# Attention scores in two PSUM banks with one maximum, one exponential and one copy for a tile, and the first key and query transposes within the projections

## The chip, the cores and the metric

The kernel runs on one core of a Trainium2 chip, as one program. The metric is device time in microseconds (us) of one execution, the median of the runs of a version. Each of the core's engines works through its own list of instructions strictly in the order in which they stand there: TensorE (PE) does matmuls and transposes, VectorE (DVE) and ScalarE (ACT) do elementwise work, reductions and copies, GpSimd (POOL) does elementwise work on SBUF, and SyncE (SP) issues most of the DMAs. An instruction at the head of a list that waits for another engine holds up all that stand behind it.

## The reference, cut to what matters

Two transformer blocks of width 1024 over 512 tokens follow one another. The change lies in the attention layer of the first block (layer 1 of 2), which has 16 query heads in 4 groups of 4 that share a key and value head, head dimension 64, and 256 context tokens in front of the 512 latent keys, 768 keys in all:

```python
qkv = h_lat @ w_qkv
q = rmsnorm(qkv[..., :Q_DIM].reshape(B, S, N_Q_HEADS, HEAD_DIM), q_g)
k = rmsnorm(qkv[..., Q_DIM:Q_DIM + KV_DIM].reshape(B, S, N_KV_HEADS, HEAD_DIM), k_g)
q, k = apply_rope(q, cos, sin), apply_rope(k, cos, sin)
kv_c = h_ctx @ w_qkv[:, Q_DIM:]              # context keys (normed, not turned) and values
k_all = jnp.concatenate([k_c, k], axis=1); v_all = jnp.concatenate([v_c, v], axis=1)
s = jnp.einsum('bqhgd,bkhd->bhgqk', q_blk * HEAD_DIM ** -0.5, k_all)
p = jax.nn.softmax(s, axis=-1)
y = jnp.einsum('bhgqk,bkhd->bqhgd', p, v_all) ... @ w_o
```

Beside it stands adaLN: `m = silu(c) @ w_mod + b_mod`, 6 x 1024 numbers that scale and shift the layer's normalized inputs. For this layer, 32 columns of 128 of them are needed only after the attention.

## The kernel before, in words

**Projections.** `gemm_tm` multiplies the token-major input by w_qkv in blocks of 512 columns: block 2 (keys and values, latent and context), then block 0 (query heads 0 to 7), then block 1 (heads 8 to 15). Weights come by DMA (`load_raw`), are split into a high part (ACT, L294) and a low part (DVE or POOL, L295), and each product is three matmuls (L353 to L355). A block of four token blocks of 128 is 192 matmuls in two weight halves, and its results leave through a handler.

**The query handler.** `q_out` takes one token block. For block 0 the chain is: square (ACT, L1597), sum (DVE, L1599), square root (ACT, L192), a few short DVE steps, scale and two rope products (DVE, L1608, L1615, L1622), rope add (POOL, L1623), high part (ACT cast, L1644), low part (POOL, L1645). For block 1 only the norm's factor is worked out and the raw values are copied (L1657); their rope follows inside the attention loop (`q_rest`, all on POOL with one ACT cast).

**Keys and queries across.** `k_stack` (L1667 to L1670) splits one key head; `k_trans` turns two token blocks of it by four PE transposes (the transposes are all L177) and casts the result (L1703); `q_trans` does the same for one query head of four token blocks (L1710). The first `k_trans` of key head 0 and `q_trans(0)`, `q_trans(1)` stand behind the projections, then eight transposes that spread silu(c) over 128 partitions (`crow`, copied by ACT, L1814).

**The attention loop.** A tile is one query head and 128 queries against 768 keys, 64 in all. In a step t the loop issues S(t), the scores (four matmuls, L1724 to L1727, in two PSUM banks of 512 and 256 columns); T(t-2), six transposes of that tile's exponentials; the maxima of t (DVE, L1733, L1734, joined at L1736); the copies out of PSUM of the transposed tile (512 columns on DVE, L1768; 256 on ACT, L1764); E(t), two exponentials with two accumulated sums (ACT, L1746, L1747); and, for each second tile, the 24 matmuls of the pair's product with the values (V, L1779). Every eight tiles a norm round divides by the sums (`norm_a` on DVE, L1787, L1788, L1790; `norm_b`, four transposes and two copies, L1800, L1801). A PSUM tile is one bank, and eight of them go round under one name, `ps`.

**AdaLN's 32 rows.** Each is a load of 512 KB (SP), a product with `crow` (POOL, L1819) and a sum (ACT, L1820). They are spread over tiles 12 to 55, each issued behind that tile's exponential.

**Order.** The code gives the order for PE within the loop; a scheduler then merges what stands in the code into one list for each engine, so that the place on ACT, DVE and POOL of work from `fill` and from the handlers is decided by it. Nothing is reordered on the chip.

Of the kernel before, what the change touches and what calls it, by code (L numbers as in the profile page):

```python
# [63 lines left out]
def build(tc, A, out, stop=None, dbg=None):  # L64
# [12 lines left out]
    psp = es.enter_context(tc.tile_pool(name="ps", bufs=8, space=bass.MemoryType.PSUM))  # L77
    drp = es.enter_context(tc.tile_pool(name="dr", bufs=1, space=bass.MemoryType.DRAM))

    ph = K()  # L80

    class phase:

# [1510 lines left out]
    def head_rstd(ps, nh):  # L1594
        w = nh * 64
        q = t2()
        S.activation(q[:, :w], ps[:, :w], AF.Square)  # L1597
        v = sm([128, nh], tag=f"hv{nh}")
        V.reduce_sum(v, q[:, :w].rearrange("p (h e) -> p h e", e=64), axis=AX.X)  # L1599
# [61 lines left out]

# [15 lines left out]
    def next_phase():  # L1677
# [7 lines left out]
    qst = [s8r() for _ in range(4)]  # L1685
    gemm_tm(wq, [0], 8, lat_h, 4, q_out)
    gemm_tm(wq, [1], 8, lat_h, 4, q_out, first=lambda: k_stack(0))


    on = [s8(), s8()]  # L1690

    def och(c):
        return on[c // 4][:, (c % 4) * 512 : (c % 4) * 512 + 512]
# [25 lines left out]
    def scores(t):  # L1719
        hd, qb = tile_of(t)  # L1720
        KT = KTs[hd // 4][1]
        qsl = QTs[hd][:, qb * 128 : qb * 128 + 128]
        pa, pb = PS(), PS()
        mm(pa, qsl, KT[:, 0:512], start=True, stop=False)  # L1724
        mm(pa, qsl, KT[:, 768:1280], start=False, stop=True)
        mm(pb[:, 0:256], qsl, KT[:, 512:768], start=True, stop=False)
        mm(pb[:, 0:256], qsl, KT[:, 1280:1536], start=False, stop=True)  # L1727
        st_[t] = [pa, pb]

    def maxima(t):  # L1730
        pa, pb = st_[t]
        mx = sm([128, 2], tag=f"amx{t % 2}")
        V.reduce_max(mx[:, 0:1], pa, axis=AX.X)  # L1733
        V.reduce_max(mx[:, 1:2], pb[:, 0:256], axis=AX.X)  # L1734
        nmx = sm([128, 1], tag=f"anm{t % 2}")
        V.tensor_scalar(nmx, mx[:, 0:1], mx[:, 1:2], -0.125, op0=ALU.max, op1=ALU.mult)  # L1736
        st_[t].append(nmx)

    def exps(t):
        hd, qb = tile_of(t)  # L1740
        pa, pb, nmx = st_[t]
        if t % 8 == 0:
            den_[hd // 2] = sm([128, 4, 2, 2], tag=f"aden{hd // 2 % 2}")
        d2 = den_[hd // 2][:, qb, hd % 2, :]
        P = hip.tile([128, 1024], F32, tag="hi", name=nm("P"))
        S.activation(P[:, 0:512], pa, AF.Exp, bias=nmx, scale=0.125, accum_out=d2[:, 0:1])  # L1746
        gate_[t] = S.activation(P[:, 512:768], pb[:, 0:256], AF.Exp, bias=nmx, scale=0.125, accum_out=d2[:, 1:2])  # L1747
        st_[t] = P

    def p_trans(t):  # L1750
        P = st_[t]
        PT = l4()
        pts = []
        for half, nk in ((0, 4), (1, 2)):
            pt = PS()
            for j in range(nk):
                kc = 4 * half + j
                transpose(pt[:, j * 128 : j * 128 + 128], P[:, kc * 128 : kc * 128 + 128])
            pts.append(pt)
        st_[t] = (PT, pts)  # L1760

    def p_evac_b(t):
        PT, pts = st_[t]
        S.copy(PT[:, 512:768], pts[1][:, 0:256])  # L1764

    def p_evac_a(t):
        PT, pts = st_[t]
        V.tensor_copy(PT[:, 0:512], pts[0])  # L1768
# [35 lines left out]
    for i in range(3):
        k_trans(0, i)
    q_trans(0)
    q_trans(1)

    crow = xc.rearrange("p c t -> p (c t)")[:, 0:1024]
    for h_ in range(2):  # L1810
        pt = PS()
        for k in range(4):
            transpose(pt[:, 128 * k : 128 * k + 128], cs[:, 4 * h_ + k, 0:1].to_broadcast([128, 128]))
        S.copy(crow[:, 512 * h_ : 512 * h_ + 512], pt)  # L1814
    adraw = {}

    def adaln_rows(j):
        w = adraw.pop(j)
        G.tensor_tensor(w, w, crow, op=ALU.mult)  # L1819
        S.activation(w, w, AF.Copy, accum_out=mod[1][:, 16 + j, 0:1])  # L1820
        if j == 31:
            m = mod[1][:, 16:48, 0]
            V.tensor_tensor(m, m, vc("b_mod", 64, 32), op=ALU.add)

    NT_ = 64
    LT, LV = 2, 3
    adt = [12 + j * 45 // 32 for j in range(32)]
    for t in range(NT_ + LV + 3):
        for j in range(32):
            if max(adt[j] - 4, 0) == t:  # L1830
                adraw[j], = load_raw(A["wmodT"][j // 2][:, j % 2 * 1024 : j % 2 * 1024 + 1024], 1024)
        if t < NT_:
            scores(t)
        if 0 <= t - LT < NT_:
            p_trans(t - LT)
# [12 lines left out]
        if u >= 8 and u % 8 == 1:  # L1848
            norm_b(u // 8 - 1)
        if t < NT_:  # L1850
            if t % 8 in (3, 5) and t < 56:
                q_trans(2 * (t // 8) + 2 + t % 8 // 5)
            kv, w = divmod(t, 16)
            if kv < 3 and w == 5:
                k_stack(kv + 1)
            if kv < 3 and w in (8, 9, 11):
                k_trans(kv + 1, {8: 0, 9: 1, 11: 2}[w])
            for j in [j for j in range(32) if adt[j] == t]:
                with tc.issue_after(gate_[t].ins), tc.issue_after(lastg[0].ins):
                    adaln_rows(j)  # L1860
# [717 lines left out]
```

## Time and profile before

| | us |
|---|---|
| median of 3 runs (lowest, highest) | 2212.08 (2210.4, 2221.37) |
| the profiled execution | 2213.96 |
| its span | 2212.1 |
| mean granted TensorE clock of it | 0.978 |
| PE, DVE, ACT, POOL busy | 2078.8, 1415.5, 1107.3, 512.2 |

The span is the time from the first to the last instruction of the trace. The busy sums are over the whole program; the change touches only the stretch from about 386 to 611 us, in which blocks 0 and 1 of the projection and the attention lie. PE is in the chain that ended last for 64% of the span. A wait in a row stands in square brackets: the idle time before the instruction, and what ended it.

### The profile page before, as it was taken

How to read it: one execution, taken by the hardware profiler on the slowest of the kernel's cores; microseconds unless marked ns; L12 is line 12 of the kernel's file. 1: busy time of each engine (PE TensorE's matmuls, PEld its weight loads, DVE VectorE, ACT ScalarE, POOL GpSimd, SP SyncE). 2: the span in 40 equal slices, each digit the busy share in tenths (PEclk: the TensorE clock that was granted, in tenths of full speed). 3: DMA queues.
4: the chain of work that ended last, by engine and by line, in shares of the span. 5: the costliest groups of instructions: out<-in, count | busy, mean ns of one | idle time of the engine just before them, and what ended most of it. 6: DMA issues, size and time to landing. Idle time of an engine off the chain costs nothing.

```text
span 2212.1 us, 32447 instructions
## 1 busy us (share of the span) xinstructions
PE 2078.8 (94%) x12305; PEld 1694.3 (77%) x12305; DVE 1415.5 (64%) x2300; ACT 1107.3 (50%) x1977; POOL 512.2 (23%) x514
## 2 busy tenths in 40 slices
PE   6869998999998999999999999999999999999997
PEld 1448767788875667776698888999878888888997
DVE  4579878678736887267757767526363568565633
ACT  3648864388836886344434434324253465343422
POOL 1011020477202313145422101014100024101011
PEclk9889999999999999999999999999999999999998
DMA  9699973124426995321123333322322213333321
GB/s 375 263 357 392 417 278 101 58 71 135 177 89 225 377 389 186 94 73 49 57 63 100 91 100 95 96 87 68 105 84 80 67 48 94 97 95 95 96 77 39
DMA packets 94096, 323.05 MB, mean 146 GB/s; under 512 B 11521, under 2 KB 17168, under 8 KB 93424
## 3 DMA queue, kind: packets, MB, share of 16 engines
q1 hardware_dynamic: 76480, 274.76, 36.5%
q0 software_dynamic: 7856, 27.92, 3.6%
q10 hardware_dynamic: 9600, 18.26, 2.3%
q8 instruction: 98, 1.61, 0.3%
q14 instruction: 62, 0.51, 0.1%
HBM read 300.63 MB, written 20.27 MB: 145 GB/s over the span
## 4 chain that ended last, share of the span: by engine, by line
PE 64%; DVE 7%; DMA 5%; POOL 3%; issue 2%; ACT 2%; DVEq 0%; POOLq 0%; ACTq 0%; SPq 0%
PE ps L353 18%; PE ps L355 18%; PE ps L354 18%; PE ps L177 3%; PE ps L1779 1%; DVE lo L295 1%; DMA s<-in_mgu_dram 1%; POOL raw L1819 1%; PE ps L2162 1%; PE ps L2313 1%; PE ps L2361 1%; DVE s L1998 1%; DMA rawx<-in_mdn_dram 1%; DVE s L1990 1%; DMA raw<-in_mgu_dram 1%
## 5 line engine op out<-in xcount | busy, mean ns | idle before, releaser
L353 PE MATMUL ps<-s,hi 128*128 128x512 f32 (+1 forms) x1440 | 512.1, 357 | 4.0 <-DVE s L1990 2.9
L354 PE MATMUL ps<-s,hi 128*128 128x512 f32 (+1 forms) x1440 | 507.4, 353 | 3.0 <-DVE s L1998 1.8
L355 PE MATMUL ps<-s,lo 128*128 128x512 f32 (+1 forms) x1440 | 508.9, 354 | 0.0
L294 ACT CAST hi<-raw 128x1024 fp32r<-128x1024 f32 x282 | 291.8, 1047 | 411.8 <-PE ps L354 330.5
L295 DVE TENSOR_TENSOR lo<-raw,hi 128x1024 fp32r<-128x1024 f32 x231 | 287.3, 1258 | 275.4 <-ACT hi L294 275.0
L295 POOL TENSOR_TENSOR lo<-raw,hi 128x1024 fp32r<-128x1024 f32 x51 | 122.9, 2409 | 870.6 <-ACT hi L294 870.6
L353 PEld LDWEIGHTS ps<-s,hi 128*128 128x128 f32 x1440 | 270.8, 188 | 46.7 <-issue 7.4
L354 PEld LDWEIGHTS ps<-s,hi 128*128 128x128 f32 x1440 | 271.6, 189 | 42.1 <-DVE s L1998 2.4
L355 PEld LDWEIGHTS ps<-s,lo 128*128 128x128 f32 x1440 | 271.6, 189 | 38.7 <-issue 0.5
L353 PE MATMUL ps<-hi,s 128*128 128x512 f32 (+1 forms) x528 | 216.7, 411 | 8.3 <-ACT hi L294 5.4
L354 PE MATMUL ps<-lo,s 128*128 128x512 f32 (+1 forms) x528 | 212.3, 402 | 2.1 <-DVE lo L295 2.1
L355 PE MATMUL ps<-hi,s 128*128 128x512 f32 (+1 forms) x528 | 211.8, 402 | 2.4 <-DVE s L1897 2.4
L355 PE MATMUL ps<-t2r,lo 128*128 128x256 f32 (+1 forms) x640 | 188.2, 294 | 0.0
L354 PE MATMUL ps<-t2r,hi 128*128 128x256 f32 (+1 forms) x640 | 187.9, 294 | 0.0
L353 PE MATMUL ps<-t2r,hi 128*128 128x256 f32 (+1 forms) x640 | 187.2, 293 | 0.0
L353 PEld LDWEIGHTS ps<-hi,s 128*128 128x128 f32 (+1 forms) x528 | 105.7, 200 | 33.7 <-ACT hi L294 7.7
L355 PEld LDWEIGHTS ps<-hi,s 128*128 128x128 f32 (+1 forms) x528 | 105.5, 200 | 28.7 <-DVE s L1897 4.0
L354 PEld LDWEIGHTS ps<-lo,s 128*128 128x128 f32 (+1 forms) x528 | 105.8, 200 | 25.0 <-DVE lo L295 2.6
L354 PEld LDWEIGHTS ps<-t2r,hi 128*128 128x128 f32 x640 | 120.8, 189 | 5.3 <-issue 2.5
L355 PEld LDWEIGHTS ps<-t2r,lo 128*128 128x128 f32 x640 | 120.8, 189 | 5.1 <-issue 2.5
L353 PEld LDWEIGHTS ps<-t2r,hi 128*128 128x128 f32 x640 | 121.1, 189 | 2.8
L295 DVE TENSOR_TENSOR lo<-s,hi 128x1024 fp32r<-128x1024 f32 x97 | 113.9, 1220 | 7.9 <-ACT hi L294 6.3
(384 smaller groups left out, 3702.8 us busy)
## 6 DMA issues: line engine op xcount, KB each, us to landing
raw<-in_up_dram SPq DMA_DIRECT2D x88, 512.0 KB
s<-in_mgu_dram SPq DMA_DIRECT2D x64, 512.0 KB
raw<-in_mgu_dram SPq DMA_DIRECT2D x44, 512.0 KB
raw<-in_down_dram SPq DMA_DIRECT2D x44, 512.0 KB
raw<-in_dilqkv_dram SPq DMA_DIRECT2D x36, 512.0 KB
s<-in_mdn_dram SPq DMA_DIRECT2D x34, 512.0 KB
raw<-in_wmodT_dram SPq DMA_DIRECT2D x32, 512.0 KB
s<-in_wmod_dram SPq DMA_DIRECT2D x30, 512.0 KB
```

What stands on the lines that cost most here:

```text
L177: return PE.transpose(dst, src, ident if idt is None else idt)
L294: S.copy(hi, raw)
L295: eng.tensor_tensor(lo, raw, hi, op=ALU.subtract)
L353: mm(ps, ahi, bhi, start=start, stop=False)
L354: mm(ps, ahi, blo, start=False, stop=False)
L355: return mm(ps, alo, bhi, start=False, stop=stop)
L1779: mm(po_[c][o : o + 64, qb * 128 : qb * 128 + 128], vview[:, kc, c // 2 * 64 : c // 2 * 64 + 64], PTs[h_][:, kc * 128 : kc * 128 + 128], s ...
L1819: G.tensor_tensor(w, w, crow, op=ALU.mult)
L1990: V.tensor_tensor(mv, mv, bc(self.rb[:, None, 0:256], [128, 2, 256]), op=ALU.mult)
L1998: V.scalar_tensor_tensor(self.h.lo(c)[:, ts], x[:, c, ts], g_, self.h.hi(c)[:, ts], op0=ALU.mult, op1=ALU.subtract)
L2162: mm(po[64 * hh : 64 * hh + 64, kb * 128 : 512], vt, at[:, o : o + n], start=(kb == 0), stop=(kb == 3), tile_position=(0, 64 * hh))
L2313: mm(pzs[hh][:, o : o + n], q.q[pp, pr * 512 + qb * 128 : pr * 512 + qb * 128 + 128], q.k[pp, pr * 512 + k1 - n : pr * 512 + k1], start=Tr ...
```

## The change

1. PSUM is laid out anew for the attention: two buffers of two banks for scores (`pz`), one of two banks for transposed tiles (`pt`), one bank for the value products (`po`) and one for the rest (`ps`). Ahead of it and behind it there are eight of one bank as before.
2. A tile has one maximum over 768 (negated in the same instruction), one exponential with one accumulated sum, and one copy, alternately by DVE (even tiles) and ACT (odd). The factor 0.125 goes into the query's gain. `norm_a` has no sum of two parts any more and its broadcast copy is on ACT.
3. Into blocks 0 and 1 of the projection come, by `fill`: the `crow` transposes, 6 of the 32 adaLN rows, the three `k_trans` of key head 0, and `q_trans(0)` and `q_trans(1)`. The other 26 rows are spread over tiles 8 to 56. Some `q_trans` and `k_trans` stand one or two tiles later.
4. The norm's factor of block 1's queries is worked out once for all four token blocks, behind the projections.

```diff
+    def PS(dt=F32, of="ps"):
+        pool, w = getattr(ph, of)
+        return pool.tile([128, 512 * w], dt, tag=of, name=nm(of))
...
+        V.tensor_scalar(qkg[:, 0, :], qkg[:, 0, :], 0.125, None, op0=ALU.mult)
...
-        rs = gsm([128, 8], tag=f"qrs{tb}")
-        V.tensor_copy(rs, head_rstd(ps, 8))
         S.copy(raw, ps)
-        qlater[tb] = (raw, rs)
+        head_sums(ps, 8, qss[:, 8 * tb : 8 * tb + 8])
+        qlater[tb] = raw
...
+    NROW = 6
+    beside = {0: [lambda: crow_half(0)], 1: [lambda: crow_half(1)]}
+    for j in range(NROW):
+        beside.setdefault(2 * j, []).append(lambda j=j: adrow_load(j))
+        beside.setdefault(2 * j + 3, []).append(lambda j=j: adaln_rows(j))
+    for i in range(3):
+        beside.setdefault(12 + i, []).append(lambda i=i: k_trans(0, i))
+    for i in range(2):
+        beside.setdefault(14 + i, []).append(lambda i=i: q_trans(i))
+    qst = [s8r() for _ in range(4)]
+    gemm_tm(wq, [0], 8, lat_h, 4, q_out, fill=next_beside, first=lambda: k_stack(0))
+    qss = gsm([128, 32], tag="qss")
+    gemm_tm(wq, [1], 8, lat_h, 4, q_out, fill=next_beside)
...
+        pz = PS(of="pz")
+        for o, n in ((0, 512), (512, 256)):
+            for p_ in (0, 768):
+                mm(pz[:, o : o + n], qsl, KT[:, p_ + o : p_ + o + n], start=p_ == 0, stop=p_ > 0)
+        st_[t] = pz[:, 0:768]
...
+        V.tensor_reduce(nmx, st_[t], axis=AX.X, op=ALU.max, negate=True)
...
-        S.activation(P[:, 0:512], pa, AF.Exp, bias=nmx, scale=0.125, accum_out=d2[:, 0:1])
-        gate_[t] = S.activation(P[:, 512:768], pb[:, 0:256], AF.Exp, bias=nmx, scale=0.125, accum_out=d2[:, 1:2])
+        gate_[t] = S.activation(P[:, 0:768], pz, AF.Exp, bias=nmx, accum_out=den_[hd // 2][:, qb, hd % 2 : hd % 2 + 1])
...
+        (S.copy if t % 2 else V.tensor_copy)(PT[:, 0:768], pt[:, 0:768])
...
-        V.tensor_tensor(rd, den[:, :, :, 0], den[:, :, :, 1], op=ALU.add)
-        V.reciprocal(rd, rd)
+        V.reciprocal(rd, den)
         rdx = t2()
-        V.tensor_copy(rdx.rearrange("p (q h e) -> p q h e", q=4, h=2),
+        S.copy(rdx.rearrange("p (q h e) -> p q h e", q=4, h=2),
...
+    banks(pz=(2, 2), pt=(1, 2), po=(1, 1), ps=(1, 1))
+    qrs = rstd_from(qss, 1.0 / 64, [128, 32], "hnq", o=gsm([128, 32], tag="qrs"))
...
-    adt = [12 + j * 45 // 32 for j in range(32)]
+    adt = {j: 8 + (j - NROW) * 50 // (32 - NROW) for j in range(NROW, 32)}
...
-                q_rest(1, t // 7, *qlater[t // 7], G)
+                q_rest(1, t // 7, qlater[t // 7], qrs[:, 8 * (t // 7) : 8 * (t // 7) + 8], G)
```

How this moves instructions shows at three places. A number behind a name is a buffer; an `x4` stands for four alike.

POOL, the list ahead of and within block 0's query chain. In before, the rope adds and low parts of the four token blocks (`t_37..`, `s_368.`) follow a weight's low part:

```order
L295 TENSOR_TENSOR lo_3761<-raw_3754,hi_3760 128x1024
L1623 TENSOR_TENSOR t_3792<-t_3793,t_3795 128x512
L1645 TENSOR_TENSOR s_3684<-t_3792,s_3684 128x8x64
L1623 TENSOR_TENSOR t_3829<-t_3830,t_3832 128x512
L295 TENSOR_TENSOR lo_3985<-raw_3978,hi_3984 128x1024
L1645 TENSOR_TENSOR s_3685<-t_3829,s_3685 128x8x64
```

In the changed kernel, the same place, where the rope add is L1637, the low part L1659, and an adaLN row's product L1732:

```order
L305 TENSOR_TENSOR lo_3780<-raw_3773,hi_3779 128x1024
L1681 COPY s_3795<-s_3795 128x6x64
L1682 TENSOR_TENSOR s_3795<-ktok,s_3795 128x6x64
L1732 TENSOR_TENSOR raw_3723<-raw_3723,xc 128x1024
L1732 TENSOR_TENSOR raw_3755<-raw_3755,xc 128x1024
L1732 TENSOR_TENSOR raw_3825<-raw_3825,xc 128x1024
L1732 TENSOR_TENSOR raw_3903<-raw_3903,xc 128x1024
L1732 TENSOR_TENSOR raw_3973<-raw_3973,xc 128x1024
L1732 TENSOR_TENSOR raw_4001<-raw_4001,xc 128x1024
L1637 TENSOR_TENSOR t_3816<-t_3817,t_3819 128x512
L1659 TENSOR_TENSOR s_3685<-t_3816,s_3685 128x8x64
L305 TENSOR_TENSOR lo_4026<-raw_4019,hi_4025 128x1024
```

All six products stand ahead of the first rope add. On ACT the sums of the first five stand ahead of the first token block's square, and the sixth between it and its square root.

PE, the end of the projections. In before the transposes of keys and queries stand behind the last matmul of token block 3 of block 1 (`ps_3915`):

```order
L355 MATMUL ps_3915<-hi_3984,s_3180 128x512
L177 MATMUL ps_4112<-ident,s_4000 128x128 x4
L177 MATMUL ps_4118<-ident,s_4000 128x128 x4
L177 MATMUL ps_4124<-ident,s_4000 128x128 x4
L177 MATMUL ps_4130<-ident,s_3684 128x128
L177 MATMUL ps_4130<-ident,s_3685 128x128
L177 MATMUL ps_4130<-ident,s_3686 128x128
L177 MATMUL ps_4130<-ident,s_3687 128x128
```

In the changed kernel the last keys (`s_3795`) and query head 0 (`ps_4098`, from all four `s_3685` to `s_3688`) stand ahead of the last twelve matmuls of token block 3 (`ps_3948`):

```order
L365 MATMUL ps_3947<-hi_4025,s_3180 128x512
L187 MATMUL ps_4092<-ident,s_3795 128x128 x4
L187 MATMUL ps_4098<-ident,s_3685 128x128
L187 MATMUL ps_4098<-ident,s_3686 128x128
L187 MATMUL ps_4098<-ident,s_3687 128x128
L187 MATMUL ps_4098<-ident,s_3688 128x128
L363 MATMUL ps_3948<-hi_4021,s_3178 128x512
L364 MATMUL ps_3948<-lo_4022,s_3178 128x512
```

So the transpose of the fourth token block of head 0 now has twelve projection matmuls behind it.

ACT, around the casts of `q_rest` (high parts of block 1's queries). In before the first of them stands behind the fifth exponential:

```order
L1764 COPY lo_4259<-ps_4265 128x256
L1746 ACTIVATE P_4275,sm_4167<-ps_4253,sm_4272 128x512
L1644 CAST s_3684<-t_4244 128x8x64
L1747 ACTIVATE P_4275,sm_4167<-ps_4254,sm_4272 128x256
L1764 COPY lo_4297<-ps_4303 128x256
L1710 CAST t2r_4321<-ps_4316 128x512
```

In the changed kernel (exponential L1794, cast L1658, copy L1806, square root L202) it stands behind the third, close behind the square root on which its input rests:

```order
L202 ACTIVATE t_4144<-g_3944,epst 128x32
L1794 ACT_TABLE_LOAD
L1794 ACTIVATE P_4161,sm_4160<-pz_4153,sm_4158 128x768
L1794 ACTIVATE P_4170,sm_4160<-pz_4163,sm_4168 128x768
L1794 ACTIVATE P_4188,sm_4160<-pz_4172,sm_4185 128x768
L1713 CAST t2r_4257<-ps_4252 128x512
L1658 CAST s_3685<-t_4210 128x8x64
L1806 COPY lo_4202<-pt_4195 128x768
```

The copy of the second tile's transposes stands behind that cast. The third such cast (`s_3687`) stands behind the seventeenth exponential; on POOL six row products, the split of a key head and four rope steps stand between the low part of `s_3686` and the rope add that it reads.

## Rows read from the trace of the kernel before

**Rows 1.** Windows. Start:end length, busy PE, PEld, DVE, ACT, POOL, granted clock, DMA share, GB/s.

```profile
386.56:431.20 44.64, 44.64 (x193) 35.96 (x192) 28.76 (x67) 15.14 (x29) 18.83 (x15) 1.00 0.22 72
431.20:443.05 11.85, 6.78 (x42) 5.77 (x40) 10.64 (x33) 7.77 (x17) 6.24 (x7) 0.86 0.00 0
443.05:610.40 167.35, 161.14 (x1520) 137.68 (x1520) 131.09 (x293) 144.01 (x416) 99.19 (x58) 0.99 0.37 128
479.08:586.56 107.48, 101.27 (x923) 84.66 (x922) 82.29 (x175) 93.89 (x267) 74.48 (x39) 0.98 0.48 162
```

**Rows 2.** Timeline of PE, 431 to 444 us. Start, duration, engine, instruction, idle before.

```profile
431.20 2.35 PE L177 MATMUL ps<-ident,s 128*128 128x128 f32 x20
...
437.90 0.50 PE L1724 MATMUL ps<-s,t2r 128*128 128x512 f32 x1 [3.48 <-ACT t2r L1710]
...
443.05 0.89 PE L177 MATMUL ps<-ident,P 128*128 128x128 f32 x6 [1.60 <-ACT P L1746]
```

**Rows 3.** Timeline of ACT, 391 to 446 us: square roots, a cast, a table load.

```profile
402.00 0.30 ACT L192 ACTIVATE sm<-sm,epst 128x8 f32<-128x8 f32 x1 [0.75 <-DVE sm L1599]
...
407.41 0.30 ACT L192 ACTIVATE sm<-sm,epst 128x8 f32<-128x8 f32 x1
...
427.36 0.62 ACT L1644 CAST s<-t 128x512 fp32r<-128x512 f32 x1 [5.26 <-POOL t L1623]
...
439.33 1.28 ACT L1746 ACT_TABLE_LOAD   x1
```

**Rows 4.** Timeline of POOL, 400 to 462 us: rope steps.

```profile
405.56 1.29 POOL L1623 TENSOR_TENSOR t<-t,t 128x512 f32<-128x512 f32 x1 [15.13 <-DVE t L1622]
407.58 1.30 POOL L1645 TENSOR_TENSOR s<-t,s 128x512 fp32r<-128x512 f32 x1 [0.73 <-PE ps L355]
...
428.06 1.29 POOL L1645 TENSOR_TENSOR s<-t,s 128x512 fp32r<-128x512 f32 x1 [0.38 <-ACT s L1644]
...
450.63 1.04 POOL L1608 TENSOR_TENSOR t<-s,g 128x512 f32<-128x512 f32 x1
...
454.50 1.29 POOL L1623 TENSOR_TENSOR t<-t,t 128x512 f32<-128x512 f32 x1
```

**Rows 5.** Timeline of PE, 481 to 491 us: scores, transposes, value products.

```profile
483.19 0.51 PE L1724 MATMUL ps<-s,t2r 128*128 128x512 f32 x1
...
484.00 0.82 PE L177 MATMUL ps<-ident,P 128*128 128x128 f32 x6
484.66 0.60 PE L177 MATMUL ps<-ident,s 128*128 128x128 f32 x4
...
486.73 1.53 PE L1779 MATMUL ps<-lo,s 128*64 128x128 f32 x24
488.19 0.66 PE L177 MATMUL ps<-ident,t 128*128 128x128 f32 x4
```

**Rows 6.** Lines by form, 437 to 612 us. Instruction and count, busy us and mean ns, idle before.

```profile
L1819 POOL TENSOR_TENSOR raw<-raw,xc 128x1024 f32<-128x1024 f32 x32 | 75.6, 2384 | 14.0 <-DMA raw<-in_wmodT_dram 9.9 <-ACT P L1747 3.6 <-ACT raw L1820 0.4
...
L1746 ACT ACTIVATE P<-ps,sm 128x512 f32<-128x512 f32 x64 | 45.1, 705 | 16.3 <-DVE sm L1736 16.0
...
L1768 DVE COPY lo<-ps 128x512 f32<-128x512 f32 x64 | 43.7, 682 | 1.7 <-PE ps L177 1.5
...
L1820 ACT ACTIVATE raw<-raw 128x1024 f32<-128x1024 f32 x32 | 34.4, 1073 | 1.7 <-POOL raw L1819 1.7
...
L1747 ACT ACTIVATE P<-ps,sm 128x256 f32<-128x256 f32 x64 | 31.0, 485 | 0.0
...
L1764 ACT COPY lo<-ps 128x256 f32<-128x256 f32 x64 | 24.6, 384 | 6.9 <-PE ps L177 6.7
...
L1669 POOL TENSOR_TENSOR s<-ktok,s 128x384 fp32r<-128x384 f32 x3 | 3.2, 1063 | 0.0
```

**Rows 7.** Timeline of DVE and of PE, 521 to 527 us.

```profile
521.54 2.13 DVE L1787 TENSOR_TENSOR sm<-sm 128x8 f32<-128x8 f32 x1
...
526.92 0.33 PE L1779 MATMUL ps<-lo,s 128*64 128x128 f32 x2 [1.71 <-DVE lo L1768]
```

More of the change, by code (lines that the diff above doesn't have):

```diff
@@ L76, in build, with banks @@
     smp = es.enter_context(tc.tile_pool(name="sm", bufs=1))
-    psp = es.enter_context(tc.tile_pool(name="ps", bufs=8, space=bass.MemoryType.PSUM))
     drp = es.enter_context(tc.tile_pool(name="dr", bufs=1, space=bass.MemoryType.DRAM))
     ph = K()
+    pse = es.enter_context(contextlib.ExitStack())
+    def banks(**n):
+        pse.close()
+        for name, (bufs, w) in n.items():
+            setattr(ph, name, (pse.enter_context(tc.tile_pool(name=nm(name), bufs=bufs, space=bass.MemoryType.PSUM)), w))
     class phase:
@@ L102, in nm @@
         return f"{p}{uid[0]}"
-    def PS(dt=F32):
-        return psp.tile([128, 512], dt, tag="ps", name=nm("ps"))
+    def PS(dt=F32, of="ps"):
+        pool, w = getattr(ph, of)
+        return pool.tile([128, 512 * w], dt, tag=of, name=nm(of))
+    banks(ps=(8, 1))
     def s8(dt=F32):
@@ L1597, in head_rstd @@
         S.activation(q[:, :w], ps[:, :w], AF.Square)
+        V.reduce_sum(v, q[:, :w].rearrange("p (h e) -> p h e", e=64), axis=AX.X)
+    def head_rstd(ps, nh):
         v = sm([128, nh], tag=f"hv{nh}")
[L1599 removed]
+        head_sums(ps, nh, v)
         return rstd_from(v, 1.0 / 64, [128, nh], f"hn{nh}")
@@ L1684, in build @@
             then=(ctx_h, 2, kv_out(0, False)))
[L1685 to L1693, printed above, removed]
     def k_trans(kvh, i):
@@ L1709, in q_trans, with crow_half, adrow_load, adaln_rows @@
         QT = t2r()
-        S.copy(QT, pt)
+        (V.tensor_copy if hd == 1 else S.copy)(QT, pt)
         QTs[hd] = QT
+    crow = xc.rearrange("p c t -> p (c t)")[:, 0:1024]
+    def crow_half(h_):
+        pt = PS()
+        for k in range(4):
+            transpose(pt[:, 128 * k : 128 * k + 128], cs[:, 4 * h_ + k, 0:1].to_broadcast([128, 128]))
+        S.copy(crow[:, 512 * h_ : 512 * h_ + 512], pt)
+    adraw = {}
+    def adrow_load(j):
+        adraw[j], = load_raw(A["wmodT"][j // 2][:, j % 2 * 1024 : j % 2 * 1024 + 1024], 1024)
+    def adaln_rows(j):
+        w = adraw.pop(j)
+        G.tensor_tensor(w, w, crow, op=ALU.mult)
+        S.activation(w, w, AF.Copy, accum_out=mod[1][:, 16 + j, 0:1])
+        if j == 31:
+            m = mod[1][:, 16:48, 0]
+            V.tensor_tensor(m, m, vc("b_mod", 64, 32), op=ALU.add)
+    NROW = 6
[7 more added lines that the diff above has]
+        beside.setdefault(14 + i, []).append(lambda i=i: q_trans(i))
+    nbeside = [0]
+    def next_beside():
+        for f in beside.get(nbeside[0], ()):
+            f()
+        nbeside[0] += 1
+    qst = [s8r() for _ in range(4)]
+    gemm_tm(wq, [0], 8, lat_h, 4, q_out, fill=next_beside, first=lambda: k_stack(0))
+    qss = gsm([128, 32], tag="qss")
+    gemm_tm(wq, [1], 8, lat_h, 4, q_out, fill=next_beside)
+    on = [s8(), s8()]
+    def och(c):
+        return on[c // 4][:, (c % 4) * 512 : (c % 4) * 512 + 512]
     st_, po_, den_, gate_ = {}, {}, {}, {}
@@ L1751, in p_trans, with p_evac @@
         P = st_[t]
[L1752 to L1768, printed above, removed]
+        pt = PS(of="pt")
+        for kc in range(6):
+            transpose(pt[:, kc * 128 : kc * 128 + 128], P[:, kc * 128 : kc * 128 + 128])
+        st_[t] = l4(), pt
+    def p_evac(t):
+        PT, pt = st_[t]
+        (S.copy if t % 2 else V.tensor_copy)(PT[:, 0:768], pt[:, 0:768])
     def pv(t):
@@ L1801, in norm_b @@
         V.tensor_tensor(och(c), po_.pop(c), rdb, op=ALU.mult)
[L1804 to L1823, printed above, removed]
+    banks(pz=(2, 2), pt=(1, 2), po=(1, 1), ps=(1, 1))
+    qrs = rstd_from(qss, 1.0 / 64, [128, 32], "hnq", o=gsm([128, 32], tag="qrs"))
     NT_ = 64
     LT, LV = 2, 3
-    adt = [12 + j * 45 // 32 for j in range(32)]
-    for t in range(NT_ + LV + 3):
-        for j in range(32):
+    adt = {j: 8 + (j - NROW) * 50 // (32 - NROW) for j in range(NROW, 32)}
+    for t in range(NT_ + LV + 2):
+        for j in adt:
             if max(adt[j] - 4, 0) == t:
-                adraw[j], = load_raw(A["wmodT"][j // 2][:, j % 2 * 1024 : j % 2 * 1024 + 1024], 1024)
+                adrow_load(j)
         if t < NT_:
@@ L1847, in build @@
                 norm_a(u // 8)
-        if u >= 8 and u % 8 == 1:
+        if u >= 8 and u % 8 == 0:
             norm_b(u // 8 - 1)
         if t < NT_:
-            if t % 8 in (3, 5) and t < 56:
-                q_trans(2 * (t // 8) + 2 + t % 8 // 5)
+            if t % 8 in (4, 6) and t < 56:
+                q_trans(2 * (t // 8) + 2 + t % 8 // 6)
             kv, w = divmod(t, 16)
@@ L1855, in build @@
                 k_stack(kv + 1)
[L1856 to L1860, printed above, removed]
+            if kv < 3 and w in (9, 10, 13):
+                k_trans(kv + 1, {9: 0, 10: 1, 13: 2}[w])
+            for j in adt:
+                if adt[j] == t:
+                    with tc.issue_after(gate_[t].ins), tc.issue_after(lastg[0].ins):
+                        adaln_rows(j)
             if t < 28 and t % 7 == 3:
-                q_rest(1, t // 7, *qlater[t // 7], G)
+                q_rest(1, t // 7, qlater[t // 7], qrs[:, 8 * (t // 7) : 8 * (t // 7) + 8], G)
+    banks(ps=(8, 1))
     phg.close()
```

29 lines of the change are left out of this document (8 added, 21 removed).

## Prediction

> **What bounds the kernel now.** I read the windows first, to cut the changed stretch into three: blocks 0 and 1 of the projection, the hand-over to the attention, the attention. [rows 1] Through the projection PE is busy 44.64 of 44.64 us: nothing is lost there, and every transpose put in between costs its own time. The hand-over, from the last projection matmul to T(0), the first transposes of exponentials, takes 11.85 us at a mean granted clock of 0.86, with PE busy 6.78. The attention takes 167.35 us from T(0) to the last value product.
>
> The timeline of PE says what the hand-over is made of [rows 2]: 28 transposes (20 of keys and queries, 8 of `crow`) from 431.20, then 3.48 us idle until the casts of queries on ACT are done, scores from 437.90, and T(0) at 443.05 behind the first exponential.
>
> For the attention the timeline gives PE's own pace at full clock, by the distance of starts [rows 5]: S 0.81 (483.19 to 484.00), T 0.66 (to 484.66), V of a pair 1.46 (486.73 to 488.19); four other transposes are 0.35 to 0.44 (0.11 each, as in T), I take 0.35. A pair of tiles is 2 x 0.81 + 2 x 0.66 + 1.46 = 4.40. Besides there are 13 query turns, 9 key turns and 8 norm rounds, 30 x 0.35 = 10.5. So PE alone needs 32 x 4.40 + 10.5 = 151.3 of the 167.35; 16 us are lost. Most of that lies in the middle: 479.08 to 586.56 is 19 pairs, 5.66 each, with ACT busy 93.9 of 107.5 us [rows 1]. There ACT is the engine to look at: a pair costs it two exponentials of two parts (2 x 1.19), two copies (2 x 0.38) and more than one row sum of 1.07 [rows 6], and the exponential then waits for a maximum that comes late (16.0 us, [rows 6]).
>
> **The change: the loop.** No operation over 768 columns stands in the trace. By the step from 256 to 512, one exponential is 0.705 + 0.22 = 0.93 (estimate; not under 0.705, not over 1.19), against 1.19 and one accumulated sum less. A copy: ACT's 256 columns take 0.384, DVE's 512 take 0.682 [rows 6], so 768 are about 0.8 on ACT and 0.95 on DVE (not under 0.68, not over 1.15). ACT's work for a pair falls from 2 x (1.19 + 0.38) = 3.1 to 2 x 0.93 + 0.8 = 2.7 and it has 26 row sums instead of 32: with one row and a third of a pair's casts 4.1 to 4.3, under PE's pace. ACT ceases to set the end.
>
> What is late next is the one buffer for transposed tiles. T of a tile can't start before the copy of the one ahead is done; before, eight banks went round and this wait didn't exist. Between two T there stand by turns one S with one matmul of V (0.87), and the rest of V with S (2.2). The copy in the shorter gap is ACT's: 0.8 and about 0.1 to get going, and up to 0.9 more if an exponential is at work. That is 0 to 0.9 for a pair; I take 0.2, near the lower end, since in the order on ACT the copy stands ahead of the next two exponentials. A pair becomes 4.60: 32 x 4.60 + 10.5 + 2 (the last tile's exponential, copy and product, which nothing covers, before as after) = 159.7, a gain of 7.6.
>
> In a norm round an addition of 8 elements took 2.13 us, and behind it PE stood idle 1.71 us for a DVE copy [rows 7]; addition and broadcast leave DVE, so such stalls go; this is part of the gain. By the Trainium skill (SBUF — State Buffer, Who interferes with whom) DVE and GpSimd hold a shared port for a whole instruction and the later one is wholly blocked, which agrees with the 2.13. The same rule speaks against six products on POOL beside the weights' low parts on DVE in the projection: by it a low part could start up to 2.38 us late, and the sum below would be up to 2 us more; no row here shows that.
>
> **The change: casts that wait on POOL.** ACT works in order; a cast of `q_rest` at its head holds up all exponentials and copies behind it. That this happens the trace shows: a cast stood 5.26 us waiting for POOL [rows 3].
> First cast. In before it had 5 tiles of time. Now it stands behind the third exponential, and its input starts only when the batched square root is there, about when the first exponential starts. POOL needs three products, a row product that stands among them, and an addition: 450.63 to 455.79 is 5.16 for the rope [rows 4], and 2.38 for the row [rows 6], 7.5. ACT gets there 3 us after: 4.5 us lost on ACT, and as much on PE, which needs the copy behind the cast.
> Third cast. POOL does between the low part of token block 1 and the rope add of 2: that low part 1.29, six rows 14.3, a key head 1.06 (without its short steps), rope 5.16 [rows 4, 6], 21.8. ACT has six tiles between the casts, three pairs 13.8 and 1.5 of turns: 15.3. Lost: 6.5. If POOL gets ahead of time in between, none; so 0 to 11 for both, and I take 11, as POOL's list is fixed and each product has a row.
> The attention then takes 159.7 + 11.0 = 170.7 against 167.35: +3.4.
>
> **The change: the hand-over.** If the queries are ready, it gains: 12 + 8 key and query transposes move inside (they cost the same there), the 3.48 idle goes; what is left behind the last matmul is the square of its result, a sum, a square root, and ACT's table load of 1.28 [rows 3]. That puts T(0) at about 439.3, 3.7 earlier.
> But six row products stand ahead of the first rope add on POOL, and the sums of five ahead of the first square on ACT. The first product needs the second `crow` copy, which ACT can do at about 396 (POOL was idle for 15.13 us before 405.56, [rows 4], so nothing else holds it). 6 x 2.38 = 14.3: the last ends at 410.3, and the first square root, 402.00 before [rows 3], comes at 412, 10 us later. From it to the end of the last low part was 402.00 to 429.35, 27.35 us [rows 3, 4]; at the least it is three periods of 5.41 (402.00 to 407.41) and a chain of 6.9 (402.00 to 408.88), 23.1. So token block 3 of the queries is ready between 435.1 and 439.4; I take 437.
> PE arrives at the transpose of query head 0 at 431.20 less twelve matmuls (44.64 / 192 x 12 = 2.8) plus 20 transposes ahead of it (2.2): 430.6. It stands there 6.4 us, and the twelve matmuls are still to come: 437.4, then 2.8 at full clock, 5.6 at half; after the idle time and the mean clock of 0.86 in the hand-over [rows 1] I take 4: 441.4. Copy and square 1.2, sum, square root and table load 2.3, exponential 0.9; scores and maximum fit beside it: T(0) at about 446.3 (443.5 to 449.5), against 443.05: +3.3.
>
> **Sum.** +3.4 + 3.3 = +6.7, and the output projection starts as late as that; with some 1 us for lower clock after the stalls, +7.7 on 2213.96, the profiled execution's own time: 2221.7. That execution is 1.9 over the median of the runs, so for the median I say 2220.
>
> **Rivals.**
> A, nothing waits on POOL: the products finish early or the chain is shorter than 18.5 us from 412, and the casts meet their inputs. Then -3.7 and -7.6: about 2201. For it speaks ACT's load in the loop, which does fall; against it the 23.1 us that the chain takes at the least.
> B, the single buffer decides: if ACT's copy of the odd tile regularly meets an exponential at work, a pair loses 0.6 instead of 0.2, 32 x 0.4 = 12.8 more: 2233. It decides from a loss of 0.35 a pair on. For it: exponential and copy are on one engine in order and 0.93 is longer than the gap; against it, the copy stands ahead of two exponentials in the list.
> C, only the casts fall away, POOL being ahead: +3.3 - 7.6 = -4.3: 2208.
>
> **How the numbers follow.** About 0.5%, 11 us, is what a measurement of this kernel can tell from no change: 2201 to 2223. My forecast 0.5, its own range 2214 to 2227; A 0.12, B 0.2, C 0.18. Half of A is faster by more than the bound, and a little more where the loop gains more than I see: 0.1. Slower: B, and the third of the forecast that lies above 2223: 0.36. The rest, 0.54, is within. The range 2203 to 2235 leaves out half of A and the far end of B.
>
> **What would show it.** Right: in PE's timeline a wait of 4 to 9 us before a transpose of queries near 431, released by POOL's low part; six row products in one block on POOL from 396 to 410; ACT idle for POOL some 4 us before the first cast of the attention and 6 before the third; pairs of 4.6 us after tile 24; exponentials of 0.9. Wrong: PE without a gap up to 433 (then A), T waiting for copies in each pair (then B), or 768 columns costing as much as the two parts, in which case ACT still sets the end and the loop gains nothing.

## The result, and the profile after

The changed kernel takes 2228.24 us (median of 6 runs, 2224.51 to 2231.93) against 2211.36 us of before, measured beside it: a ratio of 1.0070, interval 1.0052 to 1.0087, 11 to 19 us slower. The forecast of 2220 had the direction and about half of the size.

The stretch ahead of the change shifts by a few us from one execution to the next, so I count from P0, the first matmul of the attention's projections in PE's timeline: 338.02 in before, 339.61 after. T(0) lies 105.0 behind it before and 114.8 after (+9.8); from T(0) to the end of the last value product it is 167.5 before and 175.1 after (+7.6). The sum is +17.4 in these two executions; the ratio makes it 15.5.

**The hand-over.** POOL's timeline of the changed kernel (start, duration, instruction, idle before) answers to [rows 4]:

```profile
397.40 16.18 POOL L1732 TENSOR_TENSOR raw<-raw,xc 128x1024 f32<-128x1024 f32 x6
418.14 1.30 POOL L1637 TENSOR_TENSOR t<-t,t 128x512 f32<-128x512 f32 x1 [4.57 <-DVE t L1636]
...
441.19 1.27 POOL L1659 TENSOR_TENSOR s<-t,s 128x512 fp32r<-128x512 f32 x1 [0.73 <-ACT s L1658]
```

The six products stand in one block, and the first rope add comes behind it. ACT's timeline answers to [rows 3]:

```profile
414.66 0.29 ACT L202 ACTIVATE sm<-sm,epst 128x8 f32<-128x8 f32 x1
...
440.49 0.62 ACT L1658 CAST s<-t 128x512 fp32r<-128x512 f32 x1 [5.23 <-POOL t L1637]
...
449.21 0.32 ACT L202 ACTIVATE t<-g,epst 128x32 f32<-128x32 f32 x1 [0.75 <-DVE g L1609]
450.69 1.28 ACT L1794 ACT_TABLE_LOAD   x1 [1.15 <-DVE sm L1785]
451.98 0.90 ACT L1794 ACTIVATE P<-pz,sm 128x768 f32<-128x768 f32 x1
```

The first square root is 75.0 behind P0, against 64.0 before, and the last low part ends at 102.8 against 91.3. PE's timeline answers to [rows 2]:

```profile
425.74 0.76 PE L364 MATMUL ps<-lo,s 128*128 128x512 f32 x1 [3.18 <-DVE lo L305]
...
442.51 0.48 PE L187 MATMUL ps<-ident,s 128*128 128x128 f32 x1 [4.19 <-POOL s L1659]
442.64 0.78 PE L363 MATMUL ps<-hi,s 128*128 128x512 f32 x1
...
446.94 0.39 PE L365 MATMUL ps<-hi,s 128*128 128x512 f32 x1
447.18 0.60 PE L187 MATMUL ps<-ident,s 128*128 128x128 f32 x4
448.67 1.63 PE L1780 MATMUL pz<-s,t2r 128*128 128x512 f32 x8 [0.90 <-ACT t L1608]
450.14 0.60 PE L187 MATMUL ps<-ident,s 128*128 128x128 f32 x4
453.02 1.59 PE L1780 MATMUL pz<-s,t2r 128*128 128x512 f32 x4 [2.28 <-ACT P L1794]
454.42 1.48 PE L187 MATMUL pt<-ident,P 128*128 128x128 f32 x6
```

PE waits 3.18 us for a weight's low part on DVE, and 4.19 for the fourth token block's transpose. The low part's input stands behind a late query cast on ACT, and the low part itself takes 3.05 us, against 1.22 for the same one in e1 below, as POOL has begun such a subtraction just before it:

```profile
422.26 2.34 POOL L305 TENSOR_TENSOR lo<-raw,hi 128x1024 fp32r<-128x1024 f32 x1 [0.78 <-ACT hi L304]
422.63 3.05 DVE L305 TENSOR_TENSOR lo<-raw,hi 128x1024 fp32r<-128x1024 f32 x1
```

The twelve matmuls behind it follow, and the scores and T(0) behind those. S(2) at 453.02 stands ahead of T(0) and waits for the first exponential, since there are two score buffers.

**The loop.** ACT's two casts, and the PE instructions behind them:

```profile
459.83 0.62 ACT L1658 CAST s<-t 128x512 fp32r<-128x512 f32 x1 [2.64 <-POOL t L1637]
...
501.61 0.62 ACT L1658 CAST s<-t 128x512 fp32r<-128x512 f32 x1 [6.74 <-POOL t L1637]
```

```profile
461.19 0.87 PE L187 MATMUL pt<-ident,P 128*128 128x128 f32 x6 [2.05 <-ACT lo L1806]
...
502.80 0.69 PE L187 MATMUL ps<-ident,t 128*128 128x128 f32 x2 [5.70 <-ACT t L1827]
```

Three things bear on the first cast's wait, and no run parts them: it stands two exponentials further ahead; a row product of 2.39 us stands among POOL's rope steps; and POOL begins these only behind the batched square root, 2.0 us ahead of T(0), where before it began 5.0 ahead of it. The first of the steps, before and after:

```profile
438.06 1.05 POOL L1608 TENSOR_TENSOR t<-s,g 128x512 f32<-128x512 f32 x1
...
452.44 1.04 POOL L1622 TENSOR_TENSOR t<-s,g 128x512 f32<-128x512 f32 x1 [5.86 <-issue]
```

Ahead of the third cast POOL doesn't lack time either: it sat idle for ACT's second cast, and only then came the 22 us of work up to the end of the rope add (501.57):

```profile
479.41 1.29 POOL L1659 TENSOR_TENSOR s<-t,s 128x512 fp32r<-128x512 f32 x1 [12.51 <-ACT s L1658]
```

The lines of the attention by form answer to [rows 6]:

```profile
L1785 DVE TENSOR_REDUCE sm<-pz 128x1 f32<-128x768 f32 x62 | 59.3, 956 | 58.1 <-PE pz L1780 51.4 <-ACT P L1794 6.2
...
L1794 ACT ACTIVATE P<-pz,sm 128x768 f32<-128x768 f32 x64 | 57.9, 906 | 9.0 <-DVE sm L1785 8.7
...
L1806 DVE COPY lo<-pt 128x768 f32<-128x768 f32 x32 | 30.5, 952 | 13.1 <-PE pt L187 11.7
...
L1806 ACT COPY lo<-pt 128x768 f32<-128x768 f32 x32 | 25.6, 800 | 21.4 <-PE pt L187 21.4
```

One exponential of 0.906 stands where there were two of 0.705 and 0.485, and the copies take 0.80 and 0.95, as estimated. The windows answer to [rows 1]; this is the whole loop and a stretch in its second half, in which ACT has room and PE shows as busy throughout:

```profile
454.42:629.52 175.10, 164.95 (x1517) 139.66 (x1516) 99.82 (x120) 131.38 (x251) 85.32 (x54) 0.97 0.29 104
540.00:600.00 60.00, 59.95 (x558) 51.21 (x558) 35.90 (x43) 49.53 (x95) 27.13 (x13) 1.00 0.40 144
```

### The profile page after: what moved, and what is told of

It is laid out like the page before. It is cut to its first block, busy times and chain, and to the rows that moved or that the text cites. A ratio compares the mean times of both kernels' runs of the same rounds, so it can differ in the third digit from the quotient of the medians.

```text
span 2224.2 us, 32079 instructions
## 1 busy us (share of the span) xinstructions
PE 2085.6 (94%) x12305; PEld 1698.0 (76%) x12305; DVE 1379.9 (62%) x2107; ACT 1100.2 (49%) x1821; POOL 515.0 (23%) x514
## 4 chain that ended last, share of the span: by engine, by line
PE 71%; DVE 9%; DMA 7%; POOL 5%; issue 5%; ACT 3%; ACTq 0%; SPq 0%; DVEq 0%; POOLq 0%
PE ps L363 19%; PE ps L365 18%; PE ps L364 18%; PE ps L187 4%; DVE lo L305 2%; PE po L1817 2%; PE pt L187 1%; PE pz L1780 1%; POOL raw L1732 1%; DMA raw<-in_mgu_dram 1%; DMA raw<-in_wmod_dram 1%; DMA s<-in_mgu_dram 1%; PE ps L531 1%; PE ps L608 1%; PE ps L390 1%
## 5 line engine op out<-in xcount | busy, mean ns | idle before, releaser
L305 DVE TENSOR_TENSOR lo<-s,hi 128x1024 fp32r<-128x1024 f32 x97 | 113.8, 1218 | 8.3 <-ACT hi L304 6.9
```

The lines of the kernel that those rows point to most:

```text
L305: eng.tensor_tensor(lo, raw, hi, op=ALU.subtract)
```

## The experiments

P0 to T(0) and T(0) to the end are read from PE's timeline of each profiled execution; the ratio is to the kernel before, run beside it.

```
                             median   ratio   95% interval     P0-T(0)  T(0)-end
before                       2211.4   1                         105.0    167.5
changed                      2228.2   1.0070  1.0052 to 1.0087  114.8    175.1
e1  no rows beside           2218.5   1.0019  1.0001 to 1.0037  104.2    178.0
e12 three rows beside        2223.6   1.0041  1.0027 to 1.0055  109.6    179.6
e11 queries behind           2226.8   1.0055  1.0035 to 1.0075  111.5    178.8
e3  old hand-over            2214.9   1.0002  0.9985 to 1.0020  101.0    174.0
e4  old loop                 2220.2   1.0031  1.0013 to 1.0049  113.8    168.3
e2  cast later (in the code) 2225.0   1.0054  1.0036 to 1.0072  115.2    172.1
e5  cast gated               2220.2   1.0019  1.0002 to 1.0035  115.5    168.0
e6  e5, split copy           2231.8   1.0070  1.0043 to 1.0097  116.7    175.2
e7  e3, cast gated           2213.6   0.9990  0.9970 to 1.0011  102.0    172.2
e8  e7, split copy           2213.1   0.9992  0.9974 to 1.0010  102.9    173.5
e9  old hand-over, late rows 2208.8   0.9973  0.9960 to 0.9987  100.8    168.1
e10 new hand-over, late rows 2207.4   0.9970  0.9957 to 0.9984  102.2    167.3
```

**The products ahead of the query chain: e1 and e12.**

```diff
-    NROW = 6
+    NROW = 0
```

> All 32 adaLN rows back in the loop (none within the projections), the rest as changed. Theory (six products on POOL hold up block 0's query chain): first square root near 402 instead of 414.7, the waits of PE of 3.2, 0.8 and 4.2 us in block 1 go, the first transposes of exponentials (T(0)) at 440 to 443 instead of 454.4; the loop keeps its casts that wait on POOL, maybe 2 us longer with more rows in it. Time 2228 - 12 + 1 = 2217, 2212 to 2220. Rival (the single buffer for transposed tiles is what costs, the hand-over only hides in it): at least 2224.

> As changed, with three row products within the projections instead of six, the other 29 in the loop. Theory (each product holds up the query chain by its 2.4 to 2.7 us): first square root 8 us earlier and T(0) at 107 instead of 114.8; the third cast then waits for POOL 1 to 2 us longer: 2228 - 8 + 2 = 2222, 2218 to 2224. Rival (the chain is paced by something other than the products, a weight's load or low part): T(0) at 112 or later.

T(0) is 104.2, 109.6 and 114.8 behind P0 with none, three and six products: 5.4 and 5.2 for three. In e1 no wait for the queries is left, and the wait for the low part is gone too; this is its PE from the end of block 1:

```profile
435.81 0.60 PE L187 MATMUL ps<-ident,s 128*128 128x128 f32 x4
437.30 1.64 PE L1780 MATMUL pz<-s,t2r 128*128 128x512 f32 x8 [0.90 <-ACT t L1608]
438.77 0.60 PE L187 MATMUL ps<-ident,s 128*128 128x128 f32 x4
441.65 0.97 PE L1780 MATMUL pz<-s,t2r 128*128 128x512 f32 x4 [2.28 <-ACT P L1794]
```

So the products, with the sums on ACT that wait for them, are the cause of the late T(0). The size that I expected of e12 was off (8 us expected, 5.2 measured): the first square root lies 66.5, 71.2 and 75.0 behind P0 with none, three and six, so that a product moves it by 1.4 us on the mean and not by its 2.4. In the traces the loop takes part of it back, 178.0 and 179.6 against 175.1, as the rows return in it: e12's third cast waits 8.54 us for POOL against 6.74. By the ratios the two runs are 11 and 6 us below the changed kernel, so there this loss doesn't show.

**What stands behind the waiting transpose: e11.**

```diff
-    for i in range(2):
-        beside.setdefault(14 + i, []).append(lambda i=i: q_trans(i))
...
+    for i in range(2):
+        q_trans(i)
```

> As changed, with six rows within the projections, but the transposes of query heads 0 and 1 stand behind the last twelve projection matmuls. Theory: the low part of token block 3 comes as late as in the changed kernel (103 us behind the first projection matmul), but the twelve matmuls, the squares and the square root are done by then: T(0) at 109 to 111 instead of 114.8, 4 to 5 us less: 2223, 2220 to 2226. Rival (the wait for the low part is all that counts, what stands behind it is hidden): 2228.

T(0) came 3.3 earlier (111.5, just outside what I expected), but the first cast of the loop rests on POOL, whose work didn't get earlier; its wait grew by 2.1, and the loop was 3.7 longer in all. The ratio of 1.0055 isn't clear of the changed kernel's 1.0070, so the rival isn't excluded:

```profile
458.82 0.62 ACT L1658 CAST s<-t 128x512 fp32r<-128x512 f32 x1 [4.71 <-POOL t L1637]
```

**Hand-over and loop apart: e3 and e4.** e3 takes `beside` away and puts the transposes, `crow` and all rows where they were; e4 puts the functions of the loop, the norm round and the eight one-bank buffers of before into the changed kernel.

> The new loop and PSUM layout, but the first key and query transposes, crow and all 32 rows behind the projections as in the kernel before. Theory: T(0) at 443 to 446 instead of 454.4, attention 175 us as changed or 1 to 3 longer for six rows more: 2228 - 9 + 2 = 2220, 2214 to 2223, so the loop alone is slower than the kernel before by 4 to 9 us. Rival (the loop gains as much as its fewer instructions say, 7 us): 2205.

> The loop, the PSUM layout and the norm round of the kernel before, but six rows, crow, and the first key and query transposes within the projections as changed. Theory: T(0) at 451 to 455 as in the changed kernel, then an attention of 160 to 167 us (six row sums of 1.07 us less on ACT, which sets the pace there; a cast may wait on POOL): 2211 + 10 - 4 + 3 = 2220, 2215 to 2226. Rival (the hand-over costs nothing, the loop is at fault): 2206 or less.

The old loop behind the new hand-over is 0.31% slower than before, and its T(0) comes 113.8 behind P0: the hand-over's price without the new loop. The new loop behind the old hand-over is level with before (1.0002). Its T(0) even comes 4.0 us earlier than before's, but its loop takes 174.0, with the cast waits in it (1.71 and 6.25 us). Together, in the changed kernel, they cost 0.70%; that this is more than the two apart make is at the edge of the intervals, and the runs don't break it down. Both e3 and e4 keep the norm's factor worked out once for all token blocks (point 4 of the change); no run takes it out, so what it gives at the hand-over and costs at the first cast isn't known by itself.

**The casts: e2 and e5.** e2 moved the casts later in the code, and the scheduler did not follow: in ACT's list the first stands behind the second exponential instead of the third, the third still behind the seventeenth. The waits are still there, 3.28 us at the first and this one at the third:

> The ACT cast and the low part of block 1's queries stand three tiles later than their rope (two for the last), the rest as changed. Theory (ACT stands in order behind casts whose input POOL has not made): the waits of ACT of 2.6 and 6.7 us before L1658's counterpart go, with the PE waits of 2.0 and 5.7 us and what follows them: 9 us less, time 2219, 2216 to 2222. Rival (POOL is simply behind, the wait returns at the next reader of its work): under 3 us less, 2225 or more.

```profile
497.79 0.62 ACT L1664 CAST s<-t 128x512 fp32r<-128x512 f32 x1 [6.06 <-POOL t L1637]
```

So e2 says nothing of the theory. e5 holds the cast behind a named exponential:

```diff
+            if t in QPART:       # {5: 0, 10: 1, 21: 2, 26: 3}
+                with tc.issue_after(gate_[t].ins):
+                    q_parts(1, QPART[t], qroped.pop(QPART[t]))
```

> As changed, but the cast and low part of block 1's queries are held behind the exponentials of tiles 5, 10, 21 and 26 (before: the 3rd, 11th, 17th and 25th exponential), so that POOL has made their input. Theory: ACT's waits for POOL of 2.6 and 6.7 us and the PE waits behind them go; T(0) to the last value product falls from 175 to 165 to 168; time 9 less than the changed kernel's 2228: 2219, 2216 to 2222. Rival (POOL's backlog returns at the next reader): T(0) to the end still over 172, 2225 or more.

No cast waits any more, and T(0) to the end falls from 175.1 to 168.0, as the theory had it: the casts cost 7.1 net. One wait stands there that the changed kernel doesn't have, of an ACT copy, and the trace puts it down to POOL again:

```profile
515.01 0.80 ACT L1813 COPY lo<-pt 128x768 f32<-128x768 f32 x1 [3.31 <-POOL t L1636]
```

**The copy's length: e6 and e8.**

```diff
-        (S.copy if t % 2 else V.tensor_copy)(PT[:, 0:768], pt[:, 0:768])
+        S.copy(PT[:, 512:768], pt[:, 512:768])
+        V.tensor_copy(PT[:, 0:512], pt[:, 0:512])
```

> The casts held as in the run before, and the copy of a transposed tile cut as in the kernel before: 512 columns on DVE, 256 on ACT. Theory (the next transposes wait for the 768-column copy of the one buffer, 0.8 to 0.95 us): the copy takes 0.68, and the wait falls by some 0.2 us a pair: 5 to 8 us less than the run before, 2212 to 2215. Rival (what lengthens a pair from 4.4 to 4.85 is not the length of the copy, or one more instruction on ACT takes it back): within 3 us of the run before, or longer.

> The run before with the copy cut in 512 on DVE and 256 on ACT. Theory: 5 to 8 us less than it, about 2202, and under the kernel before. Rival (copy length is not what a pair loses): 2208.

My expectation fell: e6 is 7 us longer than e5 in the loop, and e8 is level with e7. In the waits of e6 from 540 to 600 us there is now one that e5 doesn't have:

```profile
DVE lo L1814 <- ACT lo L1813: 7.9, 20, 1.4
```

The program makes DVE's copy wait for a semaphore of ACT's copy of the same tile, so both stand one after the other. The runs with a split copy therefore don't tell what a shorter hold of the buffer is worth.

**Where POOL's rows go: e7, e9 and e10.** e7 is e3 with the casts held; e9 puts all 32 rows behind POOL's last query work; e10 is e9 with the change's hand-over, without rows in it:

```diff
-    adt = {j: 8 + (j - NROW) * 50 // (32 - NROW) for j in range(NROW, 32)}
+    adt = {j: 26 + j * 36 // 32 for j in range(32)}
```

> The new loop with the casts held, and the hand-over of the kernel before (transposes, crow and all rows behind the projections). Theory: hand-over as in the run with the old hand-over (101 us from the first projection matmul to T(0)), attention 174 - 7 = 167: 2215 - 7 = 2208, 2204 to 2211. Rival (the casts were no loss): 2214.

> The hand-over of the kernel before, the new loop with one 768-column copy, the casts of block 1's queries behind the exponentials of tiles 5, 12, 18 and 25, and all 32 adaLN rows only from tile 26 to 60, when POOL has no query left to turn. Theory (the new loop gains, but POOL's rows in its first half take the gain back): no wait for POOL on ACT, T(0) to the end 162 to 165 instead of 172, 8 tiles in 20.2 us throughout: 2213 - 9 = 2204, 2200 to 2208, below the kernel before. Rival (the rows in the second half make ACT set the pace again, 8 tiles in 22.5 us): 2212 or more.

> As the run before it, with the hand-over of the change (crow, first key and query transposes within the projections) but no row product there. Theory: the query chain is in time, but the tail behind the last projection matmul (square, sum, square root, table load, exponential) has no transposes beside it: 104 us from the first projection matmul to T(0) against 101 to 102, so 2 to 3 us more than that run: 2207. Rival (the moved transposes gain their 3 us): 2201.

e7 gained less than expected (0.9990, level with e3 within the intervals): without cast waits, copies and sums on ACT waited for POOL instead. With the rows late these waits go in the main, and e9 and e10 are faster than both kernels, by a little: 0.9973 and 0.9970. No run gives the late rows to the old loop, so how much of this the new loop earns isn't shown. The two differ by less than their intervals, so that the hand-over inside the projections, without rows, is worth nothing measurable here; its T(0) is 1.4 later than e9's. The loops, 168.1 and 167.3, did not get to the 162 to 165 that I expected. This is the window of e10 with most of the rows:

```profile
519.00:600.00 81.00, 80.80 (x744) 67.66 (x743) 48.16 (x59) 75.22 (x148) 60.06 (x27) 1.00 0.61 206
```

PE shows as busy throughout, ACT for 75.22 of the 81 us. That PE sets the pace there is likely but not shown, as its busy time holds waits too (the pair of tiles below).

## Why the prediction was right, and where its terms were too small

The steps held. Products in one block ahead of the first rope add, a late chain, PE waiting at the fourth transpose, twelve matmuls behind it, two casts waiting for POOL: each is in the trace at the place that the prediction names, and e1, e5, e11 and e12 take them away one by one. Five terms were mis-sized. All but the casts were too small, so the size is off by half: 2228 lies just above the forecast's own 2214 to 2227, and a result within the noise had been given more chance (0.54) than a slower kernel (0.36). That the casts were over-sized by 4 us hid as much of the rest, which was luck.

*The block of products*, 14.3 predicted, 16.18 measured. By the line's own summary four of six took 2.4 and two about 3.4:

```profile
L1732 POOL TENSOR_TENSOR raw<-raw,xc x6: 2394/2406/3379, 397.4 to 411.2; 128x1024 f32<-128x1024 f32 x6
```

In the same stretch DVE has two weights' low parts:

```profile
396.87 1.65 DVE L305 TENSOR_TENSOR lo<-raw,hi 128x1024 fp32r<-128x1024 f32 x1 [1.59 <-ACT hi L304]
407.66 1.29 DVE L305 TENSOR_TENSOR lo<-raw,hi 128x1024 fp32r<-128x1024 f32 x1 [9.14 <-ACT hi L304]
```

The first and the fifth product are the long ones by the starts of their sums on ACT, and they stand beside these two. The price of the pairing, which I had weighed as one on DVE, fell on POOL, about 1 us each time; where POOL had started first, at 422.26, it fell on DVE with 1.8. The Trainium skill (SBUF — State Buffer, Who interferes with whom) has issue order decide who is blocked, and the trace agrees: in all three the one that started later lost. No run here took the low parts away.

*The chain* from the first square root to the last low part: I took 25 between 23.1 and 27.4; it measured 27.8 (414.66 to 442.46), as long as before and beyond the upper end. That PE's results were all there sooner did not shorten it; each round ran through the in-order wait for the POOL add.

*The tail* from the last projection matmul to T(0): 4.9 predicted (441.4 to 446.3), 7.2 measured (447.18 to 454.42). The missing step is S(2), which stands ahead of T(0) on PE and, with two score buffers, waits for the first exponential; and the table load stood behind the wait for the maximum, not beside it, as S(0) had itself waited 0.90 for ACT's square. These 2.3, the 2.8 of the chain, 1.1 from the products and 0.3 on the twelve matmuls make 6.5 us of the hand-over: +3.3 predicted, +9.8 measured.

*The loop without the casts*: 159.7 predicted, with 4.60 for a pair of tiles; e5 took 168.0. A pair of the changed kernel in PE's timeline, with no turn (four transposes of a query, a key or a norm round) in it:

```profile
463.45 0.97 PE L1780 MATMUL pz<-s,t2r 128*128 128x512 f32 x4
464.26 0.82 PE L187 MATMUL pt<-ident,P 128*128 128x128 f32 x6
464.84 0.95 PE L1780 MATMUL pz<-s,t2r 128*128 128x512 f32 x4
465.71 0.43 PE L1817 MATMUL po<-lo,s 128*64 128x128 f32 x2
466.08 0.88 PE L187 MATMUL pt<-ident,P 128*128 128x128 f32 x6
466.88 1.52 PE L1817 MATMUL po<-lo,s 128*64 128x128 f32 x22
468.33 0.55 PE L187 MATMUL ps<-ident,s 128*128 128x128 f32 x3
```

From 463.45 to 468.33 it is 4.88. S, T and S take 2.26, as by their prices in [rows 5]; but V's 24 matmuls, cut here into 2 and 22, take 0.37 and 1.45 (24 in one take 1.46), and the T between them 0.80 (0.66). PE's row shows no idle time there; the row of its weight loads (PEld) shows 0.17 us of waiting for ACT's copy out of the single buffer:

```profile
466.07 0.64 PEld L187 LDWEIGHTS pt<-ident,P 128*128 128x128 f32 x6 [0.17 <-ACT lo L1806]
```

What makes the rest of the 0.48 isn't shown. That the single buffer makes it was not tested; the split copy could not show it.

This pair is not the mean. From the 33rd to the 57th exponential the changed kernel takes 60.38 us with 12 turns of 0.35, which leaves 4.68 a pair. With no row at all it is 4.78, from the 17th to the 25th of e10 (three turns); before, from the 57th to the last, also with no row, it is 4.43 (one turn):

```profile
475.64:495.83 20.19, 20.18 (x189) 17.07 (x189) 11.92 (x14) 13.38 (x25) 6.83 (x8) 1.00 0.02 5
590.14:606.00 15.86, 15.86 (x157) 14.04 (x157) 12.80 (x32) 11.57 (x39) 0.00 (x0) 1.00 0.05 12
```

So the new loop's layout and order cost some 0.3 us a pair where nothing else holds it, a little more than the 0.2 that I took. The rest of e5's 8 us is no loss in each pair: by its exponentials 4.9 of it fall between the 25th and the 33rd, where the copy at 515.01 waits, and 2.3 behind the 57th.

*The casts* were over-sized: 11 predicted, 7.1 by e5.

Of the rivals, A (nothing waits) and C (the casts meet their inputs) fell, as both waits are in the trace. B's price, 0.6 a pair, was not reached, though the loss lies about the 0.35 from which I had said that it decides.

The gain of 7.6 that the forecast put at ACT did not come: without the waits at the casts the loop takes 168.0 (e5) against 167.5 before. These windows run from the start of the 33rd exponential to that of the 57th, in before, the changed kernel, e4 (old loop) and e9 (new loop, late rows); ACT is the fourth busy sum:

```profile
522.43:590.14 67.71, 62.90 (x577) 53.23 (x576) 53.42 (x114) 57.57 (x165) 35.98 (x17) 0.97 0.54 189
544.68:605.06 60.38, 60.33 (x565) 51.42 (x561) 36.22 (x44) 50.52 (x100) 22.45 (x10) 1.00 0.42 150
538.47:597.78 59.31, 57.73 (x575) 50.99 (x573) 47.33 (x111) 53.09 (x155) 20.42 (x9) 1.00 0.50 176
522.71:585.60 62.89, 62.85 (x580) 52.90 (x578) 37.21 (x45) 58.96 (x118) 56.08 (x25) 1.00 0.54 176
```

The changed kernel is 7.3 us shorter there than before, but it has 12 row sums in the stretch and before has 17. With the same 12 the old loop of e4 is shorter still by 1.1, in one execution of each. The new loop pays where rows crowd ACT: e9 has 21 in the stretch and still takes less than before with 17.

What stays open: e9 and e10 are 6 us faster than before by their ratios, and only 3 to 4 of it lie between P0 and the end of the attention in the profiled executions; where the rest is they don't show.

## What to carry to other kernels

Work that is moved "beside" a busy engine still stands in some in-order list: before moving it, read what it is now ahead of on each engine it touches, and count that chain, not the free time of the engine. When a faster step lets consumers arrive earlier, look for the producer that was early enough only because the consumer was slow; here a cast two exponentials further ahead and a rope that begins behind a batched square root were together enough to make ACT wait for a GpSimd that had been idle before. And if an edit is meant to move an instruction, look for it in the engine's list, not in the code.

## What the runs showed of the hardware that was not expected

A POOL product of 2.4 us took 3.4 where a DVE subtraction of two SBUF operands had started before it, and such a subtraction, 1.22 us in e1, took 3.05 where one on POOL had started before it. And PE shows as busy for the whole of a stretch both at 4.78 us a pair (20.18 of 20.19 us, e10) and at 4.43 (15.86 of 15.86, before): its busy time doesn't tell whether it runs at its pace.
